# Gate and up with a third pair of K tiles in seven block products, SwiGLU's silu as one ScalarE function, and early tables in a pool of their own

## The chip, the core and the metric

The kernel runs on one core of a Trainium2 chip. It has a matrix engine (TensorE, PE in the rows, with PEld for its weight loads), VectorE (DVE), ScalarE (ACT), GpSimd (POOL) and SyncE (SP), which issues the loads. Each engine has its own list of instructions; semaphores tie the lists together. The metric is the device time of one execution in microseconds (us), lower is better. The kernel before was timed in three runs: median 1160.01 us, lowest 1159.96, highest 1160.74.

## What is computed

One layer of an encoder for 256 tokens of width 2048, in float32: a block with two kinds of attention heads, a cross attention into 256 memory tokens, a SwiGLU block and a last RMSNorm. The change touches only the SwiGLU block, whose hidden width is 5632, and the place in memory of some tables of the attention blocks:

```python
hf = rms_norm(x, g_ffn[layer])
x = x + (jax.nn.silu(hf @ w_gate[layer]) * (hf @ w_up[layer])) @ w_down[layer]
```

Here `silu(z)` is `z * sigmoid(z)`, and `w_gate` and `w_up` are 2048 x 5632.

## The kernel before

**Three products for one.** TensorE gets float32 numbers as two parts, h and l. `split_into` makes them: ScalarE casts the source to h (L99), VectorE subtracts h from the source to get l (L100). `mm` (L89 to L93) then issues three matmuls for one product: h·h, l·h and h·l. All weights of the kernel go this way: a 1 MB load into `wraw` (three buffers), casts into `wh` and subtractions into `wl` (four buffers each, 128 x 1024), matmuls of 128 x 512 columns.

**Gate and up.** The first 512 hidden columns are computed by `narrow_chunk`, the other 5120 by five calls of `wide_chunk`, 1024 columns each; the text calls them wide chunks 1 to 5. Each runs a gate projection and then an up projection, both in `wide_project`, and each of these ten projections goes over K = 2048 in eight pairs of K tiles, 0 to 7. A pair's 256 rows of K, 256 tokens and 1024 columns make a product of 2x2 blocks. A plain pair (P in `GU_KINDS`) does it with 8 block products, 24 matmuls. A summed pair (W) does it with 7 block products of sums and differences, 21 matmuls. Its activation sums are made once, in `summed_pair`; its weight sums are made by VectorE every time: `tsum`, L693 (1024 columns), L697 and L698 (512 each). A summed pair's weights are then split in four tiles: three in the `wh`/`wl` ring and one in `wh2`/`wl2`, which has one buffer. In the kernel before pairs 2 and 4 are summed.

**Banks, leave and join.** A projection gathers in eight PSUM banks: four `acc` banks, for two token halves by two column halves, and four banks Q1, Q5, Q7 and Q6 (`q` in the rows), which the summed pairs share. When the last summed pair has been multiplied, `leave` takes the Q banks out: ScalarE copies Q1 (L722), VectorE does four steps (L723 to L726). When the last pair has been multiplied, `join` adds each `acc` bank to its part (L730, four times). All four `acc` banks serve the next projection or down product too, in the same order: its first matmul writes the bank that the first join has read.

**After the joins.** The gate's result goes through a sigmoid on ScalarE (L810) and a product on VectorE (L811), the up result is multiplied with it (L818), transposed on TensorE, and split as the activations of the down product. After wide chunk 1, 3 and 5 a down product follows (`wide_add` and, at the end, `project`), after 2 and 4 the next chunk's gate projection.

**What sets the order.** Loads stay in program order. The rest of each engine's list is set at build time by a scheduler that plays the program through with its own estimate of every duration; on the chip every engine then runs its list in that order.

Of the kernel before, what the change touches and what calls it, by code (L numbers as in the profile page):

```python
# [11 lines left out]
F32 = mybir.dt.float32  # L12
# [7 lines left out]
P = 128  # L20
# [18 lines left out]
GU_KINDS = "PPWPWPPP"  # L39
# [35 lines left out]
def encoder_block(ctx: ExitStack, tc: tile.TileContext, a, out):  # L75
# [8 lines left out]
    pps = ctx.enter_context(tc.tile_pool(name="pps", bufs=4, space=PS))  # L84
    tables = ExitStack()
# [105 lines left out]
    posi = const.tile([P, NT], I32, name="posi")  # L191
    invf = const.tile([P, NF], F32, name="invf")
# [59 lines left out]
    posf = const.tile([P, NT], F32, name="posf")  # L252
# [81 lines left out]
    cosr = const.tile([P, NT, 2, DR // 2], F32, name="cosr")  # L334
    sinr = const.tile([P, NT, 2, DR // 2], F32, name="sinr")
    cosd = const.tile([P, NT, 2, DD // 2], F32, name="cosd")
    sind = const.tile([P, NT, 2, DD // 2], F32, name="sind")
# [155 lines left out]
    gdb = const.tile([P, DV], F32, name="gdb")  # L493
# [125 lines left out]
    soft_pool.close()  # L619
    wsum = ctx.enter_context(tc.tile_pool(name="wsum", bufs=1))  # L620
# [139 lines left out]
    def normalized_pairs():  # L760
# [12 lines left out]
        for i, kind in enumerate(GU_KINDS):  # L773
            xr = x2raw[i // 2][:, i % 2 * 2:i % 2 * 2 + 2, :]
            if kind == "P":
                if n == 4:
                    t, n = act_tile(name="x2n"), 0
                split_into(t[:, n:n + 2, :], xr)
                pairs.append(Pair(t[:, n:n + 2, :]))
                n += 2  # L780
            else:
                pairs.append(summed_pair(xr[:, :, :P], xr[:, :, P:]))
        return pairs

    def narrow_chunk(c):
# [5 lines left out]
        for tt in range(NT):  # L791
            r = rstdf[:, tt:tt + 1]
            sg = nat("sg")
            nc.scalar.activation(sg, ga[tt], AF.Sigmoid, scale=r)
            nc.vector.scalar_tensor_tensor(out=sg, in0=ga[tt], scalar=r, in1=sg, op0=ALU.mult, op1=ALU.mult)
            h = nat("h")
            nc.vector.scalar_tensor_tensor(out=h, in0=ua[tt], scalar=r, in1=sg, op0=ALU.mult, op1=ALU.mult)
            transposed(t, h, tt, 4)
# [4 lines left out]
    def wide_chunk(c, spare):  # L803

        g = wide_result(xn, a["w_gu"][c, 0], GU_SEQ)
        for tt in range(NT):
            for oc in range(2):
                sg = nat("sg")
                gs = g[tt][:, oc, :]
                nc.scalar.activation(sg, gs, AF.Sigmoid)  # L810
                nc.vector.tensor_tensor(out=gs, in0=gs, in1=sg, op=ALU.mult)  # L811
# [176 lines left out]
```

## Time and profile before

| | |
|---|---|
| median of three runs | 1160.01 us |
| the profiled execution | 1160.6 us |
| its span in the trace | 1158.8 us |
| TensorE matmul busy | 1149.4 us, 99% of the span, 5512 matmuls |
| VectorE busy | 900.3 us, 78% |
| ScalarE busy | 612.1 us, 53% |
| mean granted TensorE clock | 0.998 of full speed |

The span is the time between the first and the last recorded instruction; the execution's own time is 1.8 us longer. A matmul's row gives its start and a modelled length that overlaps the next one's; the distance from one start to the next is what it costs. A VectorE row overlaps the next by 0.08 us when the two run without a gap.

### The profile page before, as it was taken

The page shows a single profiled execution, that of the slowest core. Times are in us where ns is not written, and L with a number is a line of the kernel's source. Part 1 is how long each engine was busy: PE and PEld are TensorE (multiplying, and loading weights), DVE is VectorE, ACT ScalarE, POOL GpSimd, SP SyncE. Part 2 cuts the span into 40 slices and gives each one's busy share as a digit, 9 for nine tenths or more (in the row PEclk, how much of TensorE's full clock was granted, in tenths as well). Part 3 has the DMA queues.
Part 4 walks back from the last instruction along what each step waited for, and adds up shares of the span by engine and source line. Part 5 has one row for each costly group of instructions (what it writes and reads, how often), then busy time and mean ns, then how long its engine had stood idle before and what let it go on. Part 6 is the DMA issues. An engine that isn't in the chain of part 4 may idle for free.

```text
span 1158.8 us, 14403 instructions
## 1 busy us (share of the span) xinstructions
PE 1149.4 (99%) x5512; PEld 961.6 (83%) x5512; DVE 900.3 (78%) x1192; ACT 612.1 (53%) x866; POOL 69.8 (6%) x81
## 2 busy tenths in 40 slices
PE   9999999999999999999999999999999999999997
PEld 7888888888888888888888888888888888888887
DVE  7588766586867776978888787797888788798873
ACT  6755454554665565655444554564544554554552
POOL 4920000001000000000000000000000000000021
PEclk9999999999999999999999999999999999999999
DMA  9665334445754445465555555655556555565551
GB/s 349 222 205 189 125 137 166 170 146 201 279 210 182 145 147 185 177 218 183 184 213 185 205 185 191 218 180 184 200 186 217 205 181 203 188 220 207 211 198 73
DMA packets 33620, 222.13 MB, mean 192 GB/s; under 512 B 4112, under 2 KB 4752, under 8 KB 8848
## 3 DMA queue, kind: packets, MB, share of 16 engines
q1 hardware_dynamic: 32400, 217.29, 52.4%
q0 software_dynamic: 864, 3.15, 0.8%
q8 instruction: 43, 0.70, 0.2%
q10 hardware_dynamic: 288, 0.79, 0.2%
q14 instruction: 25, 0.20, 0.0%
HBM read 219.11 MB, written 2.10 MB: 191 GB/s over the span
## 4 chain that ended last, share of the span: by engine, by line
PE 98%; issue 0%; DMA 0%; DVE 0%; ACT 0%; SPq 0%; POOLq 0%; POOL 0%; DVEq 0%; ACTq 0%
PE acc L91 28%; PE acc L92 28%; PE acc L93 28%; PE q L91 2%; PE q L92 2%; PE q L93 2%; PE pt L301 2%; PE ppt L448 1%; PE psc L93 1%; PE psc L92 1%; PE psc L91 1%; PE acckv L91 0%; PE acckv L93 0%; PE acckv L92 0%; PE pt L824 0%
## 5 line engine op out<-in xcount | busy, mean ns | idle before, releaser
L99 ACT CAST wh<-wraw 128x1024 fp32r<-128x1024 f32 (+2 forms) x398 | 399.4, 1015 | 386.6 <-PE acc L93 344.4
L100 DVE TENSOR_TENSOR wl<-wraw,wh 128x1024 fp32r<-128x1024 f32 (+2 forms) x398 | 468.4, 1185 | 165.9 <-ACT wh L99 163.9
L92 PE MATMUL acc<-wl,x2n_h 128*128 128x512 f32 x480 | 185.5, 390 | 0.0
L93 PE MATMUL acc<-wh,x2n_l 128*128 128x512 f32 x480 | 185.3, 389 | 0.0
L91 PE MATMUL acc<-wh,x2n_h 128*128 128x512 f32 x480 | 160.5, 390 | 0.0
L93 PEld LDWEIGHTS acc<-wh,x2n_l 128*128 128x128 f32 x480 | 90.1, 188 | 19.0
L91 PEld LDWEIGHTS acc<-wh,x2n_h 128*128 128x128 f32 x480 | 90.1, 188 | 19.0 <-issue 0.2
L92 PEld LDWEIGHTS acc<-wl,x2n_h 128*128 128x128 f32 x480 | 90.1, 188 | 18.7
L92 PE MATMUL acc<-wl,hT_h 128*128 128x512 f32 (+1 forms) x272 | 103.7, 381 | 0.0
L93 PE MATMUL acc<-wh,hT_l 128*128 128x512 f32 (+1 forms) x272 | 103.5, 380 | 0.0
L91 PE MATMUL acc<-wh,hT_h 128*128 128x512 f32 (+1 forms) x272 | 89.4, 382 | 0.0
L92 PE MATMUL acc<-wl,x0T_h 128*128 128x512 f32 x224 | 88.2, 394 | 0.1
L93 PE MATMUL acc<-wh,x0T_l 128*128 128x512 f32 x224 | 87.9, 393 | 0.0
L91 PE MATMUL acc<-wh,x0T_h 128*128 128x512 f32 x224 | 87.7, 396 | 0.0
L99 ACT CAST wh<-tsum 128x1024 fp32r<-128x1024 f32 x56 | 58.3, 1048 | 42.5 <-DVE tsum L698 31.1
L100 DVE TENSOR_TENSOR wl<-tsum,wh 128x1024 fp32r<-128x1024 f32 x56 | 67.9, 1218 | 9.3 <-ACT wh L99 9.3
L91 PEld LDWEIGHTS acc<-wh,hT_h 128*128 128x128 f32 x272 | 51.2, 188 | 9.9 <-issue 0.2
L93 PEld LDWEIGHTS acc<-wh,hT_l 128*128 128x128 f32 x272 | 51.2, 188 | 9.6
L92 PEld LDWEIGHTS acc<-wl,hT_h 128*128 128x128 f32 x272 | 51.2, 188 | 9.5
L91 PEld LDWEIGHTS acc<-wh,x0T_h 128*128 128x128 f32 x224 | 42.3, 189 | 9.0 <-ACT wh L99 1.1
L92 PEld LDWEIGHTS acc<-wl,x0T_h 128*128 128x128 f32 x224 | 42.2, 188 | 8.3 <-DVE wl L100 0.8
L93 PEld LDWEIGHTS acc<-wh,x0T_l 128*128 128x128 f32 x224 | 42.2, 188 | 7.4
(361 smaller groups left out, 2008.4 us busy)
## 6 DMA issues: line engine op xcount, KB each, us to landing
wraw<-in_w_gu SPq DMA_DIRECT2D x80, 1024.0 KB, 4.8
wraw<-in_w_dn SPq DMA_DIRECT2D x36, 1024.0 KB, 4.8
wraw<-in_w_in SPq DMA_DIRECT2D x24, 1024.0 KB, 4.8
wraw<-in_w_out SPq DMA_DIRECT2D x16, 1024.0 KB, 4.9
wraw<-in_w_down SPq DMA_DIRECT2D x8, 1024.0 KB, 4.8
wraw<-in_w_in_lat SPq DMA_DIRECT2D x7, 832.0 KB, 7.2
wraw<-in_w_xk SPq DMA_DIRECT2D x4, 1024.0 KB, 5.8
wraw<-in_w_xq SPq DMA_DIRECT2D x4, 1024.0 KB, 4.8
```

Of the source, the lines that this page charges most:

```text
L91: nc.tensor.matmul(o, l.h, r.h, start=start, stop=False)
L92: nc.tensor.matmul(o, l.h, r.l, start=False, stop=False)
L93: nc.tensor.matmul(o, l.l, r.h, start=False, stop=stop)
L99: last_cast[0] = nc.scalar.copy(out=dst.h, in_=src).ins
L100: last_split[0] = nc.vector.tensor_tensor(out=dst.l, in0=src, in1=dst.h.bitcast(F32), op=ALU.subtract).ins
L301: nc.tensor.transpose(out=pt[:, j * P:(j + 1) * P], in_=src[:, j * P:(j + 1) * P], identity=ident)
L448: nc.tensor.transpose(out=pt[:, kt * S + tt * P:kt * S + (tt + 1) * P], in_=p[:, tt, kt * P:(kt + 1) * P], identity=ident)
```

## The change

`GU_KINDS` becomes `PPWPWPWP`: pair 6 of every gate and up projection is summed as well, with its weights laid out for that on the host. One plain pair is then left over alone, pair 7, and its activations get a tile `odd` in the pool `wsum` in place of half an `act` tile. The silu is one ScalarE function: the two VectorE products with the sigmoid (L795, and L811 twenty times) go. The tables of the attention blocks (`cosr`, `sinr`, `cosd`, `sind`, `gdb` and three small ones) move from the pool `const` to a pool `early`, which is closed before `wsum` is opened, so that `wsum` with its added tile fits.

```diff
-GU_KINDS = "PPWPWPPP"
+GU_KINDS = "PPWPWPWP"
...
+    attention = ExitStack()
+    early = attention.enter_context(tc.tile_pool(name="early", bufs=1))
...
-    cosr = const.tile([P, NT, 2, DR // 2], F32, name="cosr")
+    cosr = early.tile([P, NT, 2, DR // 2], F32, name="cosr")
...
     soft_pool.close()
+    attention.close()
     wsum = ctx.enter_context(tc.tile_pool(name="wsum", bufs=1))
...
             if kind == "P":
-                if n == 4:
+                if n == 4 and "P" in GU_KINDS[i + 1:]:
                     t, n = act_tile(name="x2n"), 0
+                elif n == 4:
+                    t = Split(*[wsum.tile([P, 2, S], F32R, name="odd" + x, tag="odd" + x, bufs=1) for x in "hl"])
+                    n = 0
                 split_into(t[:, n:n + 2, :], xr)
...
-            nc.scalar.activation(sg, ga[tt], AF.Sigmoid, scale=r)
-            nc.vector.scalar_tensor_tensor(out=sg, in0=ga[tt], scalar=r, in1=sg, op0=ALU.mult, op1=ALU.mult)
+            nc.scalar.activation(sg, ga[tt], AF.Silu, scale=r)
...
-                sg = nat("sg")
-                gs = g[tt][:, oc, :]
-                nc.scalar.activation(sg, gs, AF.Sigmoid)
-                nc.vector.tensor_tensor(out=gs, in0=gs, in1=sg, op=ALU.mult)
+                nc.scalar.activation(g[tt][:, oc, :], g[tt][:, oc, :], AF.Silu)
```

Lines behind the edits get other numbers: `mm` L91 to L93 becomes L93 to L95, `split_into` L99 and L100 becomes L101 and L102, `tsum` L693, L697 and L698 becomes L696, L700 and L701, `leave` L723 to L726 becomes L726 to L729, the join L730 becomes L733, L818 becomes L820. The program as a whole has 30 matmuls fewer. The ScalarE list has four table loads in both kernels, the last ahead of the narrow chunk's sigmoid or silu.

The lists are made anew. The first place to look at is the end of the gate projection of wide chunk 2. On VectorE there stood before, from the second step of `leave` to the first join (`wl_5914` and `wl_5944` to `wl_5982` are tiles of pairs 5 to 7, `wl_6032` and `wl_6036` of the next projection's pair 0, `acc_5704` is the first `acc` bank):

```order
L724 TENSOR_TENSOR res0_5900<-q5_5779,res1_5901 128x512
L100 TENSOR_TENSOR wl_5914<-wraw_5907,wh_5913 128x1024
L725 TENSOR_TENSOR res1_5901<-res1_5901,q7_5780 128x512
L100 TENSOR_TENSOR wl_5944<-wraw_5941,wh_5943 128x1024
L100 TENSOR_TENSOR wl_5948<-wraw_5941,wh_5947 128x1024
L726 TENSOR_TENSOR res1_5901<-q5_5779,res1_5901 128x512
L100 TENSOR_TENSOR wl_5978<-wraw_5975,wh_5977 128x1024
L100 TENSOR_TENSOR wl_5982<-wraw_5975,wh_5981 128x1024
L100 TENSOR_TENSOR wl_6032<-wraw_6029,wh_6031 128x1024
L100 TENSOR_TENSOR wl_6036<-wraw_6029,wh_6035 128x1024
L693 TENSOR_TENSOR tsum_6103<-wraw_6097 128x1024
L730 TENSOR_TENSOR res0_5900<-acc_5704,res0_5900 128x512
```

After the change the same place on VectorE reads, from the first step of `leave` to the last join (`wl_6014` is the second tile of pair 7, `wl_6056`, `wl_6060` and `wl_6090` belong to the next projection's pairs 0 and 1):

```order
L726 TENSOR_TENSOR res1_6001<-q6_5804,res0_6000 128x512
L727 TENSOR_TENSOR res0_6000<-q5_5802,res1_6001 128x512
L102 TENSOR_TENSOR wl_6014<-wraw_6007,wh_6013 128x1024
L728 TENSOR_TENSOR res1_6001<-res1_6001,q7_5803 128x512
L102 TENSOR_TENSOR wl_6056<-wraw_6053,wh_6055 128x1024
L102 TENSOR_TENSOR wl_6060<-wraw_6053,wh_6059 128x1024
L729 TENSOR_TENSOR res1_6001<-q5_5802,res1_6001 128x512
L102 TENSOR_TENSOR wl_6090<-wraw_6087,wh_6089 128x1024
L733 TENSOR_TENSOR res0_6000<-acc_5727,res0_6000 128x512
L733 TENSOR_TENSOR res0_6000<-acc_5728,res0_6000 128x512
L733 TENSOR_TENSOR res1_6001<-acc_5729,res1_6001 128x512
L733 TENSOR_TENSOR res1_6001<-acc_5730,res1_6001 128x512
```

The row kinds of `leave` and of the splits between its steps are the same in both; three splits and a `tsum` that stood between them and the first join are gone from there, since `leave` now comes two pairs later.

The second place is TensorE's list at the same point, where the next projection begins. Before, the last pair finishes its banks one after the other, and `acc_6025`, which lies where `acc_5704` lay, is first written here:

```order
L91 MATMUL acc_5706<-wh_5981,x2n_h_4379 128x512
L92 MATMUL acc_5706<-wl_5982,x2n_h_4379 128x512
L93 MATMUL acc_5706<-wh_5981,x2n_l_4380 128x512
L91 MATMUL acc_5707<-wh_5977,x2n_h_4379 128x512
L92 MATMUL acc_5707<-wl_5978,x2n_h_4379 128x512
L93 MATMUL acc_5707<-wh_5977,x2n_l_4380 128x512
L91 MATMUL acc_5707<-wh_5981,x2n_h_4379 128x512
L92 MATMUL acc_5707<-wl_5982,x2n_h_4379 128x512
L93 MATMUL acc_5707<-wh_5981,x2n_l_4380 128x512
L91 MATMUL acc_6025<-wh_6031,x2n_h_4341 128x512
```

After the change pair 7 finishes all four banks in its last eight matmuls, and `acc_6049`, which lies where `acc_5727` lay, follows at once:

```order
L93 MATMUL acc_5730<-wh_6013,oddh_4396 128x512
L94 MATMUL acc_5727<-wl_6014,oddh_4396 128x512
L95 MATMUL acc_5727<-wh_6013,oddl_4397 128x512
L94 MATMUL acc_5728<-wl_6014,oddh_4396 128x512
L95 MATMUL acc_5728<-wh_6013,oddl_4397 128x512
L94 MATMUL acc_5729<-wl_6014,oddh_4396 128x512
L95 MATMUL acc_5729<-wh_6013,oddl_4397 128x512
L94 MATMUL acc_5730<-wl_6014,oddh_4396 128x512
L95 MATMUL acc_5730<-wh_6013,oddl_4397 128x512
L93 MATMUL acc_6049<-wh_6055,x2n_h_4345 128x512
```

From the last matmul into Q1 to the next projection's first matmul there are 82 starts before and 34 after. Such counts at all ten ends, before and after: chunk 1 gate 87 and 39, up 88 and 36; chunks 2 and 4 gate and up 82 and 34 each; chunks 3 and 5 gate 96 and 52, up 88 and 38.

## Rows read from the trace of the kernel before

**Rows 1.** The page: busy times, and the shares of the chain that ended last.

```profile
PE 1149.4 (99%) x5512; PEld 961.6 (83%) x5512; DVE 900.3 (78%) x1192; ACT 612.1 (53%) x866; POOL 69.8 (6%) x81
...
PE 98%; issue 0%; DMA 0%; DVE 0%; ACT 0%; SPq 0%; POOLq 0%; POOL 0%; DVEq 0%; ACTq 0%
```

**Rows 2.** Busy us by window: chunk 2 gate, chunk 2 up, chunk 3 gate.

```profile
core 0: us, PE busy (x) PEld busy (x) DVE busy (x) ACT busy (x) POOL busy (x), PEclk, DMA share, GB/s
632.80:675.10 42.30, 42.30 (x187) 34.88 (x186) 32.65 (x37) 20.20 (x23) 0.00 (x0) 1.00 0.57 202
675.10:717.50 42.40, 42.40 (x187) 34.93 (x187) 34.37 (x40) 21.90 (x25) 0.00 (x0) 1.00 0.57 199
717.50:761.70 44.20, 44.20 (x203) 36.58 (x202) 36.44 (x48) 23.99 (x31) 0.00 (x0) 1.00 0.51 182
```

**Rows 3.** Timeline of TensorE (start, length, instruction): chunk 2 gate's last into Q1.

```profile
656.55 0.40 PE L93 MATMUL q<-wh,forms_l 128*128 128x512 f32 x1
```

**Rows 4.** The same timeline at the end of the chunk 2 gate projection.

```profile
671.30 0.62 PE L93 MATMUL acc<-wh,x2n_l 128*128 128x512 f32 x2
...
674.92 0.39 PE L93 MATMUL acc<-wh,x2n_l 128*128 128x512 f32 x1
675.15 0.39 PE L91 MATMUL acc<-wh,x2n_h 128*128 128x512 f32 x1
```

**Rows 5.** Timeline of ScalarE, same stretch; in brackets idle time and its releaser.

```profile
656.99 0.59 ACT L722 COPY res<-q 128x512 f32<-128x512 f32 x1 [1.50 <-PE q L93]
657.47 3.12 ACT L99 CAST wh<-wraw 128x1024 fp32r<-128x1024 f32 x3
661.75 1.06 ACT L99 CAST wh<-wraw 128x1024 fp32r<-128x1024 f32 x1 [1.17 <-PE acc L93]
```

**Rows 6.** Timeline of VectorE, same stretch, from the leave to the joins.

```profile
657.61 0.69 DVE L723 TENSOR_TENSOR res<-q,res 128x512 f32<-128x512 f32 x1 [0.86 <-ACT res L722]
658.40 0.69 DVE L724 TENSOR_TENSOR res<-q,res 128x512 f32<-128x512 f32 x1
659.01 1.22 DVE L100 TENSOR_TENSOR wl<-wraw,wh 128x1024 fp32r<-128x1024 f32 x1
660.14 0.68 DVE L725 TENSOR_TENSOR res<-res,q 128x512 f32<-128x512 f32 x1
660.74 2.36 DVE L100 TENSOR_TENSOR wl<-wraw,wh 128x1024 fp32r<-128x1024 f32 x2
663.01 0.69 DVE L726 TENSOR_TENSOR res<-q,res 128x512 f32<-128x512 f32 x1
663.61 1.22 DVE L100 TENSOR_TENSOR wl<-wraw,wh 128x1024 fp32r<-128x1024 f32 x1
...
672.14 1.22 DVE L693 TENSOR_TENSOR tsum<-wraw 128x1024 f32<-128x1024 f32 x1
673.28 1.28 DVE L730 TENSOR_TENSOR res<-acc,res 128x512 f32<-128x512 f32 x2
674.48 0.68 DVE L697 TENSOR_TENSOR tsum<-tsum,wraw 128x512 f32<-128x512 f32 x1
```

**Rows 7.** Timeline near the start, where TensorE waits for VectorE.

```profile
9.03 1.02 DVE L100 TENSOR_TENSOR wl<-wraw,wh 128x832 fp32r<-128x832 f32 x1 [1.69 <-ACT wh L99]
...
10.11 0.50 PE L92 MATMUL acc<-wl,x0T_h 128*128 128x512 f32 x1
...
10.45 0.40 PE L93 MATMUL acc<-wh,x0T_l 128*128 128x512 f32 x1
```

**Rows 8.** Groups by line: out<-in, count, busy us, mean ns, idle before.

```profile
L811 DVE TENSOR_TENSOR res<-res,sg 128x512 f32<-128x512 f32 x20 | 13.1, 680 | 0.0
L810 ACT ACTIVATE sg<-res 128x512 f32<-128x512 f32 x20 | 12.2, 627 | 9.1 <-DVE res L730 8.9
```

**Rows 9.** Timeline of VectorE, chunk 3 gate: first tile of pair 3.

```profile
731.51 1.22 DVE L100 TENSOR_TENSOR wl<-wraw,wh 128x1024 fp32r<-128x1024 f32 x1 [0.52 <-ACT wh L99]
```

**Rows 10.** Timeline of TensorE there: that tile's first use.

```profile
734.62 0.39 PE L92 MATMUL acc<-wl,x2n_h 128*128 128x512 f32 x1
```

More of the change, by code (lines that the diff above doesn't have):

```diff
@@ L190, in encoder_block @@
     NF = DR // 2 + DD // 2
-    posi = const.tile([P, NT], I32, name="posi")
-    invf = const.tile([P, NF], F32, name="invf")
+    posi = early.tile([P, NT], I32, name="posi")
+    invf = early.tile([P, NF], F32, name="invf")
     ident = const.tile([P, P], F32, name="ident")
@@ L247, in encoder_block @@
                 mm(acc_kv[tt][:, :LAT], x, w[:, QL:], i + k == 0, i == 7 and k == 1)
-    posf = const.tile([P, NT], F32, name="posf")
+    posf = early.tile([P, NT], F32, name="posf")
     nc.gpsimd.tensor_copy(out=posf, in_=posi)
@@ L332, in encoder_block @@
     two_pi = float(np.nextafter(np.float32(2 * math.pi), np.float32(0)))
-    cosr = const.tile([P, NT, 2, DR // 2], F32, name="cosr")
-    sinr = const.tile([P, NT, 2, DR // 2], F32, name="sinr")
-    cosd = const.tile([P, NT, 2, DD // 2], F32, name="cosd")
-    sind = const.tile([P, NT, 2, DD // 2], F32, name="sind")
+    cosr = early.tile([P, NT, 2, DR // 2], F32, name="cosr")
+    sinr = early.tile([P, NT, 2, DR // 2], F32, name="sinr")
+    cosd = early.tile([P, NT, 2, DD // 2], F32, name="cosd")
+    sind = early.tile([P, NT, 2, DD // 2], F32, name="sind")
     def latents_normalized():
@@ L492, in encoder_block @@
                                    op0=ALU.add, op1=ALU.subtract)
-    gdb = const.tile([P, DV], F32, name="gdb")
+    gdb = early.tile([P, DV], F32, name="gdb")
     tc.keep_in_program_order(nc.sync.dma_start(out=gdb, in_=a["g_diff_sub"].partition_broadcast(P)))
```

## The prediction

> **What bounds the kernel now.** I read the page first: TensorE is busy for 99% of the span, and the chain that ended last lies on it for 98%, with no share for a wait on another engine [rows 1]. So each matmul that goes is worth its step, as long as TensorE is never kept waiting. Next I read the windows of single projections: VectorE is busy for 32.65 of 42.30 us in an undisturbed gate projection and for 36.44 of 44.20 in a gate projection that also takes over the previous chunk's transposes [rows 2]. It has a reserve of 18 to 23% on average; whether that is enough depends on where its work stands in its list. So last I read the timelines of the place where one projection hands its banks to the next [rows 3 to 6].
>
> Two things are to be seen there. First the clock: it is granted in full (1.00 in the windows, which is the 2.4 GHz level), and from the last matmul into Q1 (656.55) to the next projection's first matmul (675.15) there are 82 starts: 18.60 / 82 = 0.227 us each [rows 3, 4]. Second, VectorE runs its list in order and overtakes nothing. The last matmul into the first bank starts at 671.30; a reader of PSUM can follow such a start by 0.44 (656.55 to the copy at 656.99), that is at 671.74, but the join starts at 673.28, because the `tsum` row ahead of it has to end [rows 3 to 6]. In this kernel that harms nothing: the bank is needed at 675.15, 1.2 us after the first join's end.
>
> **What goes.** Ten projections lose one plain pair's 24 matmuls and get 21: 30 matmuls, 30 x 0.227 = **6.8 us less** on TensorE, all on the path.
>
> The Trainium skill's page "TensorE: Matmul & The Clock Gate", section "Wait — 56ns, not 53.3ns?", gives 215.7 ns as the step of back-to-back matmuls of 512 columns at the full clock; by that figure 30 matmuls would be worth an estimated 6.5 us. The rows here say 227 ns for three-part float32, and the rows decide.
>
> **What is added off the path.** A summed pair costs VectorE 3 splits of 1.14 (the step between rows that touch, as 672.14 to 673.28), one of 0.60, one `tsum` of 1.14 and two of 0.60: 6.4 us, against 2.3 for a plain pair. That is 41 us more over ten projections. The twenty products with the sigmoid go from it, 20 x 0.60 = 12 us [rows 8]. The sum per gate projection stays under the window, about 36 of 41.6 us. ScalarE gets 1.5 us of casts more per projection and keeps a third of its time free [rows 2]; a silu in place of a sigmoid takes the same place in its list, has one table load like the sigmoid, and lies between the join and the up product, with a whole projection of cover, so I put it at nothing (between 0 and the 0.63 of one ACTIVATE [rows 8] for the last chunk). The moved tables cost nothing: their last readers are in the attention blocks, hundreds of us ahead of `wsum`'s first writer, and loads and bytes are the same. In the narrow chunk VectorE gets one more set of activation sums, about 2 us, and loses two products and one split, about as much: 0, bounds -0.3 to +0.5.
>
> **What is moved onto the path: the join.** `leave` now follows pair 6, so only pair 7 covers it. The start of the last matmul into Q1 is time zero. In wide chunk 2 VectorE runs, after the change, the same eight rows as before: step, step, split, step, split, split, step, split. Before, they start 1.06 after zero (ScalarE's copy of Q1 ends at 1.03) and end at 663.61 + 1.22 - 656.55 = 8.28 [rows 3, 5, 6]. The order of ScalarE's casts among them and the buffers they wait for are the same too; the last cast waits for a buffer that TensorE reads until 21 matmuls after zero, before and after (661.75 - 656.55 = 5.20 = 21 x 0.227 + 0.43). So these times carry over. Behind them stands the first join, 0.68 long and overlapping by 0.08: it ends at 8.88. The next projection's first matmul is the 34th after zero, so due at 34 x 0.227 = 7.72. When TensorE waits for VectorE, the matmul starts 0.06 after the release (9.03 + 1.02 = 10.05, then 10.11), and the step behind it is 0.34 instead of 0.227 [rows 7], so 0.17 are added. TensorE stands for 8.88 + 0.17 - 7.72 = **1.33 us**. Nothing else is left in its list, since pair 7 is done. The same rows and counts stand at four ends (chunks 2 and 4, gate and up): 5.3 us.
>
> The other six ends, by the same durations:
> - Chunk 1 up: the same rows, due at 36 x 0.227 = 8.17: 0.9 us.
> - Chunks 3 and 5 up: one row fewer ahead of the join, but its last split waits for a cast, whose buffer is read until the 25th matmul: 25 x 0.227 + 0.43 + 1.05 + 0.1 = 7.26, split to 8.48, join to 9.08, due at 38 x 0.227 = 8.63: 0.6 us each.
> - Chunk 1 gate: likewise, with the 26th matmul and due at the 39th: 0.6 us.
> - Chunks 3 and 5 gate: the first bank is complete at the 45th matmul, 10.2 + 0.44; the join is at once and ends at 11.3, due at 52 x 0.227 = 11.8: nothing.
>
> The sum is 5.3 + 0.9 + 1.2 + 0.6 = **8.0 us added**. Bounds: 0, if the scheduler's lists are run otherwise than I read them, and 11, if each of the ten ends costs 0.3 more.
>
> First told by rows, VectorE does not pass a waiting row by (the join at 673.28 above); the Trainium skill's page "TensorE: Matmul & The Clock Gate", section "Architectural detail: the array is 16× 32×32, not 1× 128×128", says the same as a rule: the queues of ACT and DVE are strict first in, first out. Were it otherwise, the join would end at 34 - 7 = 27 matmuls + 0.44 + 0.68 = 7.3, ahead of 7.72, and by that the added sum would be 0. The trace agrees with the rule.
>
> **The gates of chunks 3 and 5.** There VectorE also makes the up product and splits its transposes. Before, the first tile of pair 3 is ready at 732.73 and used at 734.62, 1.9 us of reserve [rows 9, 10]. After, the joins lie some 2 us later against TensorE. From the first join's end, 0.2 ahead of the gate's first matmul: three joins, a `tsum`, a split, four L820, two `tsum` of 512 come to 7.4; then a wait to 8.65 for a cast; then 8.2 us of splits and sums to that tile's end at 16.9. TensorE wants it at about 16.7: 0.4 us with the restart, for each of the two. I take 0.8 together; bounds 0 and 4.
>
> **Sum.** 1160.6 - 6.8 + 8.0 + 0.8 = 1162.6 for a profiled execution; that of before is 0.6 above the median, so the forecast is **1162.1 us**: the gain is given back at the ends of the projections, and a little more.
>
> **Rivals.**
> 1. *The joins are in time and the gain stays.* All or most of 6.8 us: 1153.2, or 1156.6 if half the ends wait. For it: the list was made by a scheduler that saw no better place for the join, and before the change no end waits. Against it: the eight rows ahead of the join take 8.3 us at four ends before, to 0.01 us alike, and TensorE is due at 7.7.
> 2. *Slower: VectorE becomes the bound inside the gates of chunks 3 and 5.* With three summed pairs its rows there come to 38.6 us in 43.1. Its reserve at pair 3 falls from 1.9 us below zero, as above, and does not come back, since each summed pair takes 6.4 us against 4.8 of matmuls. Price: up to 2 us for each gate, and the same again where the down product behind it starts late: 1163 to 1167. It decides if the splits of pair 3 in these gates end over 0.5 us after their due time. Against it: a plain pair between two summed ones gives 5.4 us for 2.3, and TensorE's own waits at the joins give VectorE time.
> 3. *The change does not do what it says*, because silu needs table loads in every chunk. The built list has four loads, as before; no chance worth a number.
>
> **How the numbers follow.** The forecast with its own spread (1160.3 to 1163.9, from 0.2 us more or less at each of the ends) has 0.65, rival 1 has 0.13, rival 2 has 0.22. A measurement of this kernel can tell some 0.2%, 2.3 us, from no change: under 1157.7 is faster, over 1162.3 slower. The forecast lies near that border: of its 0.65 I give 0.44 to no change and 0.21 to slower; rival 2 is slower by all of its chance, rival 1 faster by all of its. So faster 0.13, same 0.44, slower 0.43. The range leaves out most of rival 1 below and the far end of rival 2 above: 1157.0 to 1165.0.
>
> **What would show it.** TensorE has 5482 matmuls and a step of 0.227. Its waits appear as idle time ahead of weight loads into `acc`, released by VectorE's L733: 1.2 to 1.4 us four times, 0.5 to 1.0 four times, 8 us in all, where the trace of before has none. VectorE's eight rows end 8.3 us after the last matmul into Q1. The prediction is wrong if the joins start before the split ahead of them ends, if these waits come to under 4 us, or if TensorE waits for over 2 us on `wl` in the gates of chunks 3 and 5. A chain of waits that still lies on TensorE alone, with a span near 1152, would be rival 1.

## The result: slower by 0.4%, and the profile after

| | before | after |
|---|---|---|
| median of five runs, us | 1160.5 | 1165.18 (1164.05 to 1166.03) |
| ratio, 95% interval | | 1.0041 [1.003, 1.0052] |
| profiled execution: span, us | 1158.8 | 1162.9 |
| TensorE matmuls | 5512 | 5482 |
| VectorE busy, us | 900.3 | 931.6 |

The forecast was 1162.1 us in 1157.0 to 1165.0, so the time lies 3 us above the forecast and just outside the range. By the bound of 0.2% it is "slower", to which the prediction gave 0.43, one hundredth less than to "same".

The page of the changed kernel, busy times and the chain that ended last, beside [rows 1]:

```profile
PE 1146.6 (99%) x5482; PEld 954.4 (82%) x5482; DVE 931.6 (80%) x1226; ACT 629.1 (54%) x888; POOL 70.8 (6%) x81
...
PE 92%; DVE 3%; issue 2%; DMA 1%; ACT 1%; SPq 0%; DVEq 0%; POOLq 0%; POOL 0%; ACTq 0%
```

Thirty matmuls went, and the chain has left TensorE for 8% of the span: VectorE, casts and loads stand in it now. But look at TensorE's busy time. Where matmuls follow each other without a gap, busy time is the sum of their steps. It fell by 1149.4 - 1146.6 = 2.8 us, and thirty steps are 6.8. That is a hint and no more, since a matmul's modelled length (0.39 us) covers a part of each wait and the start of the program differs too; the rows below show that there are two losses, and that only one of them is a wait.

The same three windows as in [rows 2], chunk 2 gate, chunk 2 up and chunk 3 gate:

```profile
core 0: us, PE busy (x) PEld busy (x) DVE busy (x) ACT busy (x) POOL busy (x), PEclk, DMA share, GB/s
632.80:675.91 43.11, 42.14 (x185) 34.21 (x183) 35.80 (x40) 22.85 (x25) 0.00 (x0) 1.00 0.56 197
675.91:719.13 43.22, 42.25 (x183) 34.27 (x184) 36.16 (x40) 23.71 (x28) 0.00 (x0) 1.00 0.55 195
719.13:762.90 43.77, 43.77 (x200) 36.12 (x201) 41.22 (x53) 24.32 (x32) 0.00 (x0) 1.00 0.55 194
```

The first two windows got longer by 0.8 us although they have three matmuls fewer: TensorE is idle for 1.0 us in each, and its busy time hardly fell. The granted clock is 1.00 throughout, the 2.4 GHz level. VectorE is busy for 41.22 of 43.77 us in the third.

**The first loss: the wait at the join.** The end of the chunk 2 gate projection, on VectorE and then on TensorE (in brackets idle time and its releaser), beside [rows 4, 6]:

```profile
667.94 0.69 DVE L726 TENSOR_TENSOR res<-q,res 128x512 f32<-128x512 f32 x1 [0.86 <-ACT res L725]
668.74 0.69 DVE L727 TENSOR_TENSOR res<-q,res 128x512 f32<-128x512 f32 x1
669.34 1.22 DVE L102 TENSOR_TENSOR wl<-wraw,wh 128x1024 fp32r<-128x1024 f32 x1
670.48 0.68 DVE L728 TENSOR_TENSOR res<-res,q 128x512 f32<-128x512 f32 x1
671.07 2.35 DVE L102 TENSOR_TENSOR wl<-wraw,wh 128x1024 fp32r<-128x1024 f32 x2
673.34 0.68 DVE L729 TENSOR_TENSOR res<-q,res 128x512 f32<-128x512 f32 x1
673.94 1.21 DVE L102 TENSOR_TENSOR wl<-wraw,wh 128x1024 fp32r<-128x1024 f32 x1
675.08 2.47 DVE L733 TENSOR_TENSOR res<-acc,res 128x512 f32<-128x512 f32 x4
```

```profile
666.89 0.40 PE L95 MATMUL q<-wh,forms_l 128*128 128x512 f32 x1
...
669.17 1.09 PE L93 MATMUL acc<-wh,oddh 128*128 128x512 f32 x4
...
674.54 0.40 PE L95 MATMUL acc<-wh,oddl 128*128 128x512 f32 x1
675.91 0.47 PE L93 MATMUL acc<-wh,x2n_h 128*128 128x512 f32 x1 [0.97 <-DVE res L733]
676.21 0.39 PE L94 MATMUL acc<-wl,x2n_h 128*128 128x512 f32 x1
```

These are the eight rows of the prediction. The last matmul into Q1 starts at 666.89; the eighth row ends 8.27 us later (8.28 forecast), the first of the four joins that read as one row starts at 675.08, ends at 675.76, and TensorE goes on at 675.91, 1.37 after its last start where 0.23 is a step.

**The second loss: longer steps.** In the same rows, from 669.17 to 674.54, stand pair 7's 24 matmuls. 5.37 / 23 = 0.2333 us a step, not 0.227. The clock is at 1.00 and no row names a wait: every single step is longer. To see all of both losses I took the starts of successive matmuls from the narrow chunk on (3212 before, 3182 after). Steps over 0.3 us, less 0.2267 each, are waits; what all other 512-column steps have over 0.2267 is the second loss:

| us | waits | longer steps |
|---|---|---|
| before | 1.4 | 3.4 |
| after | 10.0 | 6.0 |

The 1.4 of before are no real waits but single steps of 0.31 to 0.32. So the difference of the two traces is -6.8 (30 matmuls) + 8.6 (waits) + 2.6 (longer steps) - 0.45 (the narrow chunk began that much earlier in this execution) + 0.15 (rest) = 4.1 us, which is the difference of the spans.

### The profile page after: what moved, and what is told of

Same layout as the page of the kernel before. It is cut to its first block, busy times and chain, and to the rows that moved or that the text cites. A ratio compares the mean times of both kernels' runs of the same rounds, so it can differ in the third digit from the quotient of the medians.

```text
span 1162.9 us, 14414 instructions
## 1 busy us (share of the span) xinstructions
PE 1146.6 (99%) x5482; PEld 954.4 (82%) x5482; DVE 931.6 (80%) x1226; ACT 629.1 (54%) x888; POOL 70.8 (6%) x81
## 4 chain that ended last, share of the span: by engine, by line
PE 92%; DVE 3%; issue 2%; DMA 1%; ACT 1%; SPq 0%; DVEq 0%; POOLq 0%; POOL 0%; ACTq 0%
PE acc L93 25%; PE acc L94 25%; PE acc L95 25%; PE q L93 3%; PE q L94 3%; PE q L95 3%; PE pt L303 2%; DVE wl L102 1%; PE ppt L450 1%; PE psc L94 1%; PE psc L95 1%; PE psc L93 1%; DVE res L733 1%; DMA wraw<-in_w_gu 1%; ACT wh L101 0%
## 5 line engine op out<-in xcount | busy, mean ns | idle before, releaser
L101 ACT CAST wh<-wraw 128x1024 fp32r<-128x1024 f32 (+2 forms) x398 | 395.6, 1004 | 368.1 <-PE acc L95 328.0
L102 DVE TENSOR_TENSOR wl<-wraw,wh 128x1024 fp32r<-128x1024 f32 (+2 forms) x398 | 463.3, 1173 | 137.0 <-ACT wh L101 134.3
L94 PE MATMUL acc<-wl,x2n_h 128*128 128x512 f32 x320 | 125.3, 391 | 0.1
L95 PE MATMUL acc<-wh,x2n_l 128*128 128x512 f32 x320 | 125.0, 391 | 0.0
L93 PE MATMUL acc<-wh,x2n_h 128*128 128x512 f32 x320 | 107.2, 392 | 4.7 <-DVE res L733 4.7
L95 PE MATMUL acc<-wh,hT_l 128*128 128x512 f32 (+1 forms) x272 | 103.1, 380 | 0.0
L102 DVE TENSOR_TENSOR wl<-tsum,wh 128x1024 fp32r<-128x1024 f32 x76 | 91.9, 1219 | 13.9 <-ACT wh L101 13.8
L101 ACT CAST wh<-tsum 128x1024 fp32r<-128x1024 f32 x76 | 79.0, 1048 | 37.8 <-DVE tsum L701 24.1
L93 PE MATMUL acc<-wh,hT_h 128*128 128x512 f32 (+1 forms) x272 | 90.9, 382 | 1.1 <-DVE res L733 1.1
L93 PE MATMUL acc<-wh,x0T_h 128*128 128x512 f32 x224 | 87.0, 393 | 1.0 <-ACT wh L101 1.0
L95 PE MATMUL acc<-wh,x0T_l 128*128 128x512 f32 x224 | 88.0, 393 | 0.0
L93 PEld LDWEIGHTS acc<-wh,x2n_h 128*128 128x128 f32 x320 | 60.1, 188 | 19.7 <-issue 6.2
L94 PEld LDWEIGHTS acc<-wl,x2n_h 128*128 128x128 f32 x320 | 60.1, 188 | 13.5 <-DVE wl L102 1.2
L95 PEld LDWEIGHTS acc<-wh,x2n_l 128*128 128x128 f32 x320 | 60.1, 188 | 12.7
L93 PEld LDWEIGHTS acc<-wh,hT_h 128*128 128x128 f32 x272 | 51.2, 188 | 12.2 <-issue 2.3
L94 PE MATMUL q<-wl,forms_h 128*128 128x512 f32 x152 | 59.6, 392 | 0.0
L95 PEld LDWEIGHTS acc<-wh,hT_l 128*128 128x128 f32 x272 | 51.2, 188 | 9.7
L95 PE MATMUL q<-wh,forms_l 128*128 128x512 f32 x152 | 58.9, 392 | 0.0
L696 DVE TENSOR_TENSOR tsum<-wraw 128x1024 f32<-128x1024 f32 x38 | 46.4, 1220 | 8.7 <-DMA wraw<-in_w_gu 8.1
```

The source lines that it names most:

```text
L93: nc.tensor.matmul(o, l.h, r.h, start=start, stop=False)
L94: nc.tensor.matmul(o, l.h, r.l, start=False, stop=False)
L95: nc.tensor.matmul(o, l.l, r.h, start=False, stop=stop)
L101: last_cast[0] = nc.scalar.copy(out=dst.h, in_=src).ins
L102: last_split[0] = nc.vector.tensor_tensor(out=dst.l, in0=src, in1=dst.h.bitcast(F32), op=ALU.subtract).ins
L696: nc.vector.tensor_tensor(out=t[:, 0:2, :], in0=raw[:, 1:3, :], in1=raw[:, 0:1, :].to_broadcast([P, 2, 512]), op=ALU.add)
```

## The experiments

Each run has its own runs of the kernel before beside it, at 1160.3 us.

**Why are the steps longer? The same program in other places.** The edit moves three pools to the top of the memory, so that all others lie lower:

```diff
-    const = ctx.enter_context(tc.tile_pool(name="const", bufs=1))
+    const = ctx.enter_context(tc.tile_pool(name="const", bufs=1, side="right"))
...
-    sb = ctx.enter_context(tc.tile_pool(name="sb", bufs=2))
-    small = ctx.enter_context(tc.tile_pool(name="small", bufs=4))
+    sb = ctx.enter_context(tc.tile_pool(name="sb", bufs=2, side="right"))
+    small = ctx.enter_context(tc.tile_pool(name="small", bufs=4, side="right"))
```

On the changed kernel:

> The changed kernel with the same instructions in the same order on every engine; only the pools of constants, of small tiles and of the VectorE/ScalarE scratch move to the top of the on-chip memory, so that odd, wh2 and wl2 lie some 37 KB per partition lower (odd at 169,696 instead of 206,688 bytes, or near it). Question: why are TensorE's steps 0.233 to 0.236 us, not 0.2267, where a matmul reads odd, wh2 or wl2 (about 560 steps)? Theory A, place: the tile's place in the memory does it. Then these steps fall to 0.2275 on average, about 2.6 us go, and the time is 1162.0 to 1163.0 (1165.2 before this edit); the waits at the joins stay as they are (7.2 us). Theory B, neighbourhood: these steps are slow because the other engines are busiest there. Then nothing moves: 1164.5 to 1166.

Measured 1160.41 us, ratio 1.0002 [0.9993, 1.0011]: 4.8 us less than the changed kernel, nearly twice what I had expected. TensorE's timeline at the same pair 7:

```profile
667.75 1.07 PE L93 MATMUL acc<-wh,oddh 128*128 128x512 f32 x4
...
672.96 0.39 PE L95 MATMUL acc<-wh,oddl 128*128 128x512 f32 x1
674.50 0.47 PE L93 MATMUL acc<-wh,x2n_h 128*128 128x512 f32 x1 [1.14 <-ACT wh L101]
```

5.21 / 23 = 0.2267. The longer steps fell from 6.0 to 0.9 us in all, not only those on `odd`, `wh2` and `wl2` but their neighbours' too. The waits grew by 0.6: the join ends 8.87 us after the last matmul into Q1, as in the changed kernel, and TensorE is there sooner. (The row names a cast; the join ends at 674.35, 0.15 ahead of the matmul, as in the changed kernel, so it is the join.) On the kernel before:

> The kernel before with the same move of pools and no other edit. Theory A, place: about 240 steps on wh2 and wl2 lose 5 to 6 ns each, 1.1 us: 1159.0 to 1159.8 beside 1160.5, and with the run above the distance between the two kernels falls from 4.7 to about 3.2 us. Theory B: 1160.0 to 1161.0, no step changes.

Measured 1157.67 us, 0.9978 [0.9969, 0.9986], 2.7 us less where I had expected 1.1; its longer steps fall from 3.4 to 0.5. One stretch of 19 starts in chunk 2's first summed pair, in the kernel before and then in this one:

```profile
643.66 0.40 PE L91 MATMUL acc<-wh,forms_h 128*128 128x512 f32 x1
...
647.84 0.39 PE L93 MATMUL q<-wh,forms_l 128*128 128x512 f32 x1
```

```profile
642.96 0.39 PE L91 MATMUL acc<-wh,forms_h 128*128 128x512 f32 x1
...
647.04 0.39 PE L93 MATMUL q<-wh,forms_l 128*128 128x512 f32 x1
```

4.18 / 18 = 0.2322 against 4.08 / 18 = 0.2267. So the longer steps stood in the trace of before, in the very pairs of which the change makes one more. Every engine runs the same instructions in the same order, and only the places differ, so the place does it and not what the other engines do beside it.

**Which places?** I first took it for the height. The kernel before, with the pool `wp` of the weight tiles put high and all others low:

```diff
-    wp = ctx.enter_context(tc.tile_pool(name="wp", bufs=3))
...
-    sb = ctx.enter_context(tc.tile_pool(name="sb", bufs=2))
-    small = ctx.enter_context(tc.tile_pool(name="small", bufs=4))
+    sb = ctx.enter_context(tc.tile_pool(name="sb", bufs=2, side="right"))
+    small = ctx.enter_context(tc.tile_pool(name="small", bufs=4, side="right"))
+    wp = ctx.enter_context(tc.tile_pool(name="wp", bufs=3, side="right"))
```

> The kernel before with the same instructions in the same order and other places: the pool of the weight tiles is moved so that wh lies at 179,392 to 195,776 bytes of a partition, wl at 195,776 to 212,160, and wh2, wl2, tsum lie below 153,088. Theory A, place (a tile that lies high costs TensorE steps, whoever else is busy): the steps with a wl operand, one of three, take 5 to 9 ns more in the whole program, from its first projection on: about 1800 x 6.5 ns = 12 us, 1168 to 1176, and the steps on wh2 are no longer slow. By the tile it is seen from which address on. Theory B, something else about wh2, wl2 and odd (their pool, their moment): about 1157.7, as with the low tiles.

Measured 1183.78 us in a single run, 23 us more than before and beyond what either theory said. The page:

```profile
PE 1171.4 (99%) x5512; PEld 959.0 (81%) x5512; DVE 901.8 (76%) x1192; ACT 612.6 (52%) x866; POOL 68.6 (6%) x81
```

TensorE's timeline, 24 starts in plain pairs of chunk 2's gate:

```profile
651.05 0.39 PE L91 MATMUL acc<-wh,x2n_h 128*128 128x512 f32 x1
...
656.41 0.39 PE L93 MATMUL acc<-wh,x2n_l 128*128 128x512 f32 x1
```

5.36 / 23 = 0.233. Every step of a plain pair is longer, whether it streams `wl` at 195,776 bytes and above or `wh` at 179,392. Yet in the low layout of before `wh2` lay at 180,352 and its steps were 0.2267. Height can't be it. What fits is where the tile that TensorE streams (a weight tile) starts against the tile that it loads (activations), whole multiples of 512 bytes left out, since all slices of a tile lie such multiples apart:

| layout | start of the weight tile | of the activations | step, us |
|---|---|---|---|
| before, plain pairs | 0 | 0 | 0.2267 |
| before, stretch with `wh2` (6 of its 21 matmuls) | 288 | 0 | 0.232 |
| after, pair 7 with `odd` | 64 | 352 | 0.233 |
| both low layouts, all pairs | 128 | 128 | 0.2267 |
| `wp` high, plain pairs | 192 | 0 | 0.233 |

Starts are those that the program gives its tiles. The test leaves the tiles high and moves them by 224 bytes:

```diff
     wsum = ctx.enter_context(tc.tile_pool(name="wsum", bufs=1))
+    wsum.tile([P, 56], F32, name="pad", bufs=1)
```

> The changed kernel with one unused tile of 224 bytes ahead of the others in the pool wsum; no instruction changes. What a high place alone cannot explain: with wh at 179,392 bytes the steps were slow (0.2333 us), with wh2 at 180,352 to 188,544 they were not (0.2267). The rule that fits all five layouts so far: a step is slow where the tile that TensorE streams (wh, wl, wh2, wl2) and the tile that it loads (activations) start at different places within a line of some hundred bytes. In the changed kernel wh, wl and the activations start at 64 past a multiple of 512, odd, wh2 and wl2 at 352 past; the pad brings all to 64. Theory A2, offset: the slow steps go although the tiles lie high, 1160 to 1161.5, as with the low tiles. Theory A, height: nothing moves, 1164 to 1166.

Measured 1161.02 us, 1.0009 [1.0, 1.0018]; longer steps 1.1 us in all, and pair 7's 24 matmuls take 673.43 - 668.21 = 5.22, 0.2267 a step. Height falls, offset stands. (The profiled execution has 2 us more of waits than the low layout, nearly all of it at the start of the up projections of chunks 3 and 5; the medians differ by 0.6.) Then 32 bytes between the buffers of `wh` and of `wl`, in the low layout of before:

```diff
-                w = [wp.tile([P, 1024], F32R, name=x, tag=x, bufs=4)[:, :n * ncols].rearrange("p (k c) -> p k c", k=n)
+                w = [wp.tile([P, 1032], F32R, name=x, tag=x, bufs=4)[:, :n * ncols].rearrange("p (k c) -> p k c", k=n)
```

> The kernel before with the low tiles and 32 bytes between the buffers of wh and of wl, so that the eight buffers start 256, 224, 192, 160, 128, 96, 64 and 32 bytes ahead of the activations' place within 4,096; no instruction changes. Theory A2, offset: the steps differ by buffer. If 128 bytes is the period, the first wh and the first wl (256 and 128 ahead) stay at 0.2267 us and the other six cost 4 to 9 ns more: some 3500 to 4500 steps x 6.5 ns, 1175 to 1188. If the period is 256, only the first wh is fast; if 512 or more, none is: up to 1195. Theory A, height: all lie low, 1157.7.

Measured 1177.63 us in a single run, TensorE busy 1165.4 us against 1146.6 without the gaps. By buffer, the mean step is longer by 3.7 to 7.2 ns, and none of the eight is fast. That does not settle the period, because a step next to a slow one is longer too, as the stretch above shows: `wh2` and `wl2` still start where the activations do in this run, and their steps, between slow ones, are 3.9 ns longer as well. A buffer that would be fast by itself would not show it. The period stays open, and so does what it is in the chip that compares the two places.

**Why do the joins come late? Their place in VectorE's list.** The rule added to the changed kernel, with the first join (`held` is that of the projection before, `n` counts the pairs, and `issue_after` sets the order on the engine without a wait):

```diff
+        held, first_join[0] = first_join[0], None
...
+            if n == 1 and held is not None:
+                behind.enter_context(tc.issue_after(held))
+            if n == 3:
+                behind.close()
...
-            nc.vector.tensor_tensor(out=y, in0=Q[5], in1=v, op=ALU.add)
+            last_step[:] = [lambda: nc.vector.tensor_tensor(out=y, in0=Q[5], in1=v, op=ALU.add)]
...
+            if (tt, oc) == (0, 0):
+                first_join[0] = done.ins
+                with tc.issue_after(done.ins):
+                    last_step[0]()
```

> The changed kernel with one rule added to VectorE's order: the fourth step of leave, and everything of the next projection from its second pair on, stand behind the first join. So the first join stands right behind the second split of the next projection's first pair. My theory (VectorE's order at the ends makes TensorE wait): by the rows of the changed kernel the split ends 6.54 us after the last matmul into Q1, the bank is complete at 27 x 0.227 + 0.44 = 6.57, and the join ends at 7.25, ahead of 7.72: the waits of 1.14 (four ends), 0.66, and 0.46 (three ends) go, 6.7 us in all with the longer step behind each, and the time is 1158 to 1160. Rival: the waits only move (to the second bank, or to the splits that now stand behind the join): 1162 to 1165. If the bank itself, not the order, is late, nothing moves.

Measured 1163.4 us, 1.0028 [1.0017, 1.0039]: 1.8 us less than the changed kernel, and the rival's range. The waits at the first bank are all gone, so the order did cause them. The end of chunk 1's gate shows where they went, VectorE first:

```profile
523.74 0.69 DVE L741 TENSOR_TENSOR res<-acc,res 128x512 f32<-128x512 f32 x1 [0.58 <-PE acc L95]
524.35 0.68 DVE L737 TENSOR_TENSOR res<-q,res 128x512 f32<-128x512 f32 x1
524.95 1.22 DVE L102 TENSOR_TENSOR wl<-wraw,wh 128x1024 fp32r<-128x1024 f32 x1
526.08 1.22 DVE L704 TENSOR_TENSOR tsum<-wraw 128x1024 f32<-128x1024 f32 x1
527.22 1.88 DVE L741 TENSOR_TENSOR res<-acc,res 128x512 f32<-128x512 f32 x3
```

```profile
524.94 0.39 PE L93 MATMUL acc<-wh,x2n_h 128*128 128x512 f32 x1
...
526.99 0.39 PE L93 MATMUL acc<-wh,x2n_h 128*128 128x512 f32 x1
527.95 0.50 PE L93 MATMUL acc<-wh,x2n_h 128*128 128x512 f32 x1 [0.58 <-DVE res L741]
```

The first join starts 0.43 after the start of its bank's last matmul, and TensorE goes straight on at 524.94. Then a split and a `tsum`, held back until here, step ahead of the second join, and the second bank is 0.7 late. So the rule was widened, with the low tiles, to two joins, as here, and then to all four, with (1, 1) in its place and the fourth step of `leave` behind the second join:

```diff
-            if (tt, oc) == (0, 0):
+            if (tt, oc) == (0, 1):
                 first_join[0] = done.ins
```

> The changed kernel with the low tiles, and with what the next projection sends VectorE from its second pair on kept behind the first two joins (the fourth step of leave behind the first). Where the joins alone were put first, seven waits at the first bank went, but five came at the second bank, whose join then stood behind a split and a tsum (0.7, 0.3, 0.7, 0.3, 0.7 us and 0.11 for the step behind each). Theory (what stands ahead of each join on VectorE decides, bank by bank): these go too; left are the third banks of the gates of chunks 3 and 5, 0.6 us each. 1160.4 of the low kernel less 7.7 of its waits, plus 1.2 and some 1 for work that now comes later: 1153.5 to 1156. Rival (VectorE has no reserve left, so a wait taken away at one bank comes back at another place): 1157 to 1160.

Measured 1157.98 us, 0.9977 [0.9967, 0.9987]. Again the rival's range: the second banks are in time, but TensorE now waits in the gates of chunks 3 and 5 ahead of pairs 5 and 7, at the first bank behind these gates, and in the up projections that follow (0.2 to 0.6 us each).

> As the run with two joins, but behind all four joins (the fourth step of leave behind the second). Theory: the third banks of the gates of chunks 3 and 5 are then in time too; the splits of pair 1 come some 1.5 us later, with 3 us to spare: 1153 to 1155. Rival (no reserve): TensorE waits on wl instead, ahead of pairs 1 to 3 of the next projection, and the time is 1156 to 1160.

Measured **1154.82 us**, 0.9949 [0.9937, 0.9962], as the theory had it, and faster than both kernels. VectorE at the chunk 2 gate, with the joins right behind the second split:

```profile
671.68 2.35 DVE L102 TENSOR_TENSOR wl<-wraw,wh 128x1024 fp32r<-128x1024 f32 x2
674.05 1.29 DVE L741 TENSOR_TENSOR res<-acc,res 128x512 f32<-128x512 f32 x2
675.26 0.68 DVE L737 TENSOR_TENSOR res<-q,res 128x512 f32<-128x512 f32 x1
```

The chain on its page:

```profile
PE 97%; DMA 1%; ACT 1%; issue 0%; SPq 0%; DVE 0%; POOLq 0%; POOL 0%; DVEq 0%; ACTq 0%
```

The chain is back on TensorE; waits fell from 10.7 to 4.8 us. The largest that is left, 1.4 us, stands in chunk 1's down product. I laid it to the rule at the end of chunk 1's up projection, lifted the rule there, and put the pad in place of the low tiles:

> The two causes taken away together and the tiles left high: the changed kernel with the 224-byte pad and with the joins first as in the run with all four joins, except at the end of chunk 1's up projection (ahead of the first down product), where that order cost 2.6 us and the old one 0.9. Theories offset and order together: 1154.8 - 1.7 = 1153 (1152.3 to 1154), 0.6% under the kernel before. If the height counts as well: 1156 to 1158.

Measured 1154.88 us, 0.9952 [0.9939, 0.9966], 1.9 above the 1153 expected. The pad does as much as the low tiles beside this order too, so height counts for nothing once more; but the wait in chunk 1's down product stayed, so the rule at that end is not its cause. The rows of the low run with all four joins point to another, on VectorE and then on TensorE:

```profile
600.22 0.68 DVE L767 TENSOR_TENSOR xres<-xres,v 128x512 f32<-128x512 f32 x1
600.82 1.28 DVE L770 TENSOR_TENSOR xres<-xres,acc 128x512 f32<-128x512 f32 x2
```

```profile
600.05 0.39 PE L95 MATMUL acc<-wh,hT_l 128*128 128x512 f32 x1
601.65 0.47 PE L93 MATMUL acc<-wh,hT_h 128*128 128x512 f32 x1 [1.21 <-ACT wh L101]
```

Here the first half of the down product hands its banks to the second. The row names a cast, but the first of the two joins (L770) ends at 601.50, 0.15 ahead of the matmul, as at the joins above; its bank was complete at about 599.1, and the last steps of the down product's own `leave` (L767 is the last) stand ahead of it. So by its rows this is the same loss, at an end that the rule leaves out; no run takes it away.

**More cover instead of another order.** Pairs 5 and 6 change places, with the low tiles:

```diff
-    GU_SEQ = list(range(len(GU_KINDS)))
+    GU_SEQ = [0, 1, 2, 3, 4, 6, 5, 7]
```

> The changed kernel with the low tiles and pairs 5 and 6 in the other order: kinds P P W P W W P P, so that two plain pairs stand behind the last summed one. Theory (too little cover behind leave is what made the joins late): the first join has 24 matmuls, 5.4 us, more, and VectorE 2.3 us more in front of it, so no wait at the ends, 1160.4 - 7.7 = 1152.7; but two summed pairs in a row ask 12.8 us of VectorE in 9.6 us of TensorE, with one buffer of wh2: I expect 0.5 to 1.5 us of waits on wl or wh2 in each of the ten projections, 1158 to 1167. Rival: VectorE's lead of some us at that place covers it: 1152 to 1155.

Measured 1160.38 us, 0.9997 [0.9988, 1.0006]: no gain over the low layout. Most waits at the ends are gone (1.0 at one and 0.7 at two are left), and in the gates of chunks 3 and 5 the second of the two summed pairs waits instead. TensorE's windows there:

```profile
742.00:743.90 1.90, 0.79 (x4) 0.29 (x2) 1.83 (x3) 1.09 (x2) 0.00 (x0) 1.00 0.00 0
743.91:746.60 2.69, 2.23 (x7) 1.48 (x8) 2.69 (x4) 2.69 (x4) 0.00 (x0) 0.92 0.00 0
746.60:749.60 3.00, 3.00 (x9) 2.35 (x8) 3.00 (x4) 2.52 (x3) 0.00 (x0) 0.50 0.86 289
749.60:752.00 2.40, 2.40 (x12) 1.97 (x11) 2.05 (x2) 0.09 (x1) 0.00 (x0) 1.00 1.02 406
```

TensorE is idle for 1.1 of the first 1.9 us and for 0.5 of the next 2.7, and behind that the granted clock is 0.50, the 1.2 GHz level, for 3 us: a step is 0.43 there, 0.2 more than at full clock, and eight such steps cost another 1.6 us in each of the two gates.

**The silu alone, and pair 6 without it.** First the changed kernel with `GU_KINDS = "PPWPWPPP"`:

> The kernel before with the silu as one ScalarE function and the early tables in their own pool, but with pairs 2 and 4 summed as before. My step: worth nothing by itself, since VectorE had a reserve and no wait; 1159.5 to 1161.0, the same as before, with 1.5 us of idle time at most moved on VectorE. Rival: the function itself or a table load costs time at the narrow chunk or in each chunk, 0.5 to 1.3 us for each load: over 1162.

Measured 1160.28 us, 1.0001 [0.9992, 1.0009]: nothing, as forecast. The trace has the same four table loads of 1.28 us as before. Then the changed kernel with the sigmoid and its products back (the narrow chunk's too; that part of the edit is left out here):

```diff
-                nc.scalar.activation(g[tt][:, oc, :], g[tt][:, oc, :], AF.Silu)
+                sg = nat("sg")
+                gs = g[tt][:, oc, :]
+                nc.scalar.activation(sg, gs, AF.Sigmoid)
+                nc.vector.tensor_tensor(out=gs, in0=gs, in1=sg, op=ALU.mult)
```

> The changed kernel with the sigmoid and its product on VectorE as before (20 products of 0.60 us more on VectorE): only the third summed pair and the early pool are left of the change. By my reckoning these products stand behind the joins, and VectorE has a reserve of some 4 us in each gate projection and of next to none in the gates of chunks 3 and 5: the products of a gate run in the up projection, so the waits grow little, by 0 to 3 us: 1165 to 1168. Rival (VectorE has no reserve left anywhere): all 12 us show, 1170 to 1178. Rival (the scheduler finds a better list by chance): 1160 to 1164.

Measured 1169.48 us, 1.008 [1.0067, 1.0093], between the two ranges that I gave. So the silu is worth nothing beside two summed pairs and 4.3 us beside three. It spares VectorE 12 us, of which a third shows; but the lists are made anew as well, so it is not VectorE's time alone. More than half of what the profiled execution waits longer is at one place, the end of chunk 1's gate, where the new list puts a `tsum`, a split and the fourth step of `leave` ahead of the join. On TensorE:

```profile
527.27 0.47 PE L93 MATMUL acc<-wh,x2n_h 128*128 128x512 f32 x1 [2.22 <-DVE res L733]
```

And in windows around it, columns as above:

```profile
523.00:524.64 1.64, 1.64 (x8) 1.31 (x7) 1.14 (x2) 0.34 (x1) 0.00 (x0) 1.00 0.90 295
527.27:529.00 1.73, 1.73 (x6) 1.43 (x7) 1.73 (x3) 1.12 (x2) 0.00 (x0) 0.81 0.03 9
529.00:531.70 2.70, 2.70 (x8) 2.09 (x7) 2.70 (x5) 1.23 (x2) 0.00 (x0) 0.50 0.39 103
531.70:533.00 1.30, 1.30 (x7) 1.09 (x6) 1.30 (x4) 1.05 (x1) 0.00 (x0) 0.98 0.99 416
```

A wait of 2.4 us at the join, where the changed kernel has 0.5, and behind it 3 us at the 1.2 GHz level, which cost another 1.5.

## Why the prediction was wrong, step by step

- **What goes: the failing step.** "All on the path" held, and the count too (5482). But the prediction put every matmul at 0.227 us, worked out over 82 starts of plain pairs [rows 3, 4]. The step is not the same in all pairs: 0.2322 around `wh2` already in the kernel before, and 0.2333 in pair 7, whose activations the change puts into `odd`. Of the 2.6 us that the prediction left out, `odd` takes 1.5 (24 matmuls in ten projections, 6.4 ns each), and the ten more stretches with `wh2` and `wl2` and the neighbours of both the rest. The term for the matmuls should have been -4.2, not -6.8. The runs with the pad and with both low layouts show that the places cause it. The prediction said that the moved tables cost nothing because their readers are long done; that is right for their contents, but it never asked where `odd` comes to lie.
- **The join: right in mechanism, place and size.** VectorE's eight rows end after 8.27 (8.28 forecast) and the join after 8.87 (8.88) at the four ends of chunks 2 and 4. The waits with the longer step behind them are 1.22 there (1.33 forecast), because TensorE comes late itself: 24 longer steps put its due time from 7.72 to 7.88. Against that the release was dearer than forecast: 0.15 from the join's end to the matmul and 0.08 in the step behind it, where the prediction took 0.06 and 0.11 from a wait on a `wl` tile [rows 7]. At the other ends 0.74 in place of 0.9, 0.54 in place of 0.6 three times, and nothing at the first bank behind the gates of chunks 3 and 5. The sum is 7.25 against 8.0. The run with the first join ahead took just these waits away, which shows that the order causes them.
- **VectorE overtakes nothing.** The prediction set this against the row of the `tsum` in [rows 6]. It holds here: in the rows of the chunk 2 gate the bank is complete at 673.14 + 0.44 = 673.6, and the join stands behind two more rows until 675.08.
- **The gates of chunks 3 and 5: twice the size, another place.** Forecast 0.8 together, inside these gates, ahead of the first tile of pair 3. There TensorE does not wait (no step is over 0.33 us). The waits come one projection later, at the start of the up projections (from 762.90 and 1022.32): 0.3 and 1.2 us, at the second bank in chunk 5 and in pair 1 in both. TensorE at the start of chunk 5's up projection:

```profile
1023.69 0.39 PE L93 MATMUL acc<-wh,x2n_h 128*128 128x512 f32 x1
1024.56 0.50 PE L93 MATMUL acc<-wh,x2n_h 128*128 128x512 f32 x1 [0.49 <-DVE res L733]
...
1028.03 0.50 PE L94 MATMUL acc<-wl,x2n_h 128*128 128x512 f32 x1
```

  On VectorE a `tsum` stands ahead of the second join and had waited 0.87 for a load:

```profile
1022.68 1.23 DVE L696 TENSOR_TENSOR tsum<-wraw 128x1024 f32<-128x1024 f32 x1 [0.87 <-DMA wraw<-in_w_gu]
1023.82 0.68 DVE L733 TENSOR_TENSOR res<-acc,res 128x512 f32<-128x512 f32 x1
```

- **The sum.** Forecast 1162.6 for a profiled execution. Put right by the rows: + 2.6 for the steps, - 0.75 at the joins, + 0.7 behind the two gates, - 0.45 for the earlier start is 1164.7, which is the span with 1.8 around it. The median of five runs is another 0.5 above that execution.
- **The rivals.** The first (joins in time) is out: no run of the given order shows it. The second (slower, VectorE the bound in the gates of chunks 3 and 5) had its time right, 1163 to 1167, but its mechanism accounts for 1.5 us at most, and none of it inside the gates; VectorE's rows there came to 41.2 us where it had 38.6. The third is out by the silu run. None of the three was the one that came: a fourth, by which the new matmuls are dearer than the old ones.
- **The chances.** They leaned on a forecast whose spread took in every unknown wait and no unknown step, since the step seemed the best known number of all.

The Trainium skill has one fixed step for matmuls in a row: its page "TensorE: Matmul & The Clock Gate", section "Wait — 56ns, not 53.3ns?", gives the columns over 2.4 GHz and some 2.5 ns, 215.7 ns for 512 columns. The runs show two values, 226.7 and 233, at a granted clock of 1.00, and the measurement decides. The page's figure does stand in the changed kernel's trace, in two of its warm-up matmuls (L187, 512 columns of bfloat16), which start 217 and 216 ns apart; what makes the kernel's float32 matmuls 10 ns longer even where their places agree, no run here tests. The Trainium skill's page "SBUF — State Buffer", section "Who interferes with whom", counts two independent read ports for TensorE and says that "PE and ACT never wait on anyone". So far the runs agree: with the same work on every other engine, the longer steps came and went with the places alone. But by the runs the places of the two tiles that TensorE itself reads do matter to each other, 6.4 ns for each matmul, whatever the ports are.

## What to carry to other kernels

Before a product is traded for cheaper ones, compare the step of the matmuls that go with the step of those that come, pair by pair from their starts: a step that is longer at full clock and without a wait points to where the operands lie, and 224 unused bytes or another order of pools may be worth more than the change. When a late step is moved nearer to the end of a stage, list what stands ahead of the instruction that releases the next stage's bank on its in-order engine; if it is work that nobody needs yet, hold all of it back, since holding it behind the first release only moves the wait to the next. With both put right the change pays: 1154.82 us, 2.85 under the kernel before with its tiles put right (1157.67) and 5.5 under the kernel before as it was.

## What the runs showed of the hardware

- With weight tiles and activations at the same place within 512 bytes throughout, TensorE's step for 128 x 512 float32 columns is 226.7 ns in plain and summed pairs; at the other distances tried (32 to 256 bytes in steps of 32, and 288) it is 230 to 234 on average, 233.3 in stretches where every matmul is 192 or 288 bytes off. A step between longer ones is some 4 ns longer itself, though its own tiles agree. With the whole ring of weight tiles 192 bytes off (a single run) the program took 1183.78 us, 26 more than with all places equal (1157.67).
- How high the tiles lie made no difference: `odd` at 206,912 bytes is as fast as at 172,160.
- After idle times of 1.1 and 0.5 us close together, and after one of 2.2, the granted clock was 0.50 for some 3 us; after the single idle times of 1.0 us at the joins of the changed kernel, and after one of 1.2 with all four joins first, it stayed at 1.00.
